# Results of tiles 46 and 47 in four small transfers, and the move of tile 40 in one piece

## The chip, the cores and the metric

The kernel runs on one core of one Trainium2 chip. The metric is the device time of one execution in microseconds (us). Before the change it is 209.26 us, the median of three runs (209.13 to 209.33). A core has five engines that work side by side, each with its own list of instructions: TensorE (PE in the profile, its weight loads PEld), VectorE (DVE), ScalarE (ACT), GpSimd (POOL) and SyncE (SP). They wait for each other by semaphores. Data go between the device memory and the core's own memory by transfers (DMA), which an engine issues and sixteen DMA engines carry out. In the core's own memory a tensor lies in 128 rows, the partitions.

## The reference

The kernel computes a batched matrix product, scaled, plus a second tensor:

```
batch, m, k, n = 16, 512, 1024, 768
out = (scale * np.matmul(x, weight) + add_value).astype(np.float32)
```

`x` is 16 x 512 x 1024, `weight` 1024 x 768, `add_value` and the output 16 x 512 x 768, all float32; `scale` is 0.1. The read inputs are 61.87 MB and the written output 25.17 MB.

## The kernel before

The 16 x 512 rows of `x` are one matrix of 8192 x 1024. It is worked on in 64 tiles of 128 rows. The tiles lie in three blocks (`BLOCKS`): tiles 0 to 23, 24 to 47 and 48 to 63. Inside a block, row p of every tile comes from partition p, and the rows of successive tiles follow each other in device memory: in the block of 24 tiles, partition p holds 24 successive rows of the matrix. A transfer of n successive tiles is therefore 128 rows, each of one unbroken stretch of n x 4096 bytes for `x` and n x 3072 bytes for `add_value` and the output.

`STREAM` lists the transfers in the order in which SyncE issues them. `x40+8` is the load of `x` for tiles 40 to 47, `a` stands for `add_value`, `w` for the weights and `o` for results that leave. `sync_engine` (the page's L106 is the wait, L113 to L118 the issues) waits before each one for the transfer eight places earlier (the eight semaphores in `lanes`), for the room it writes to, and for results for the results it sends. The last entry, `o60+4`, is issued after the section that holds all the other work (`tile_critical`), behind a barrier of all engines (L237).

- `xs` has room for 16 tiles of `x`. `ao` has room for 32 tiles; a tile of `add_value` is loaded there, the result is computed in place, and the result leaves from there.
- `mover` runs on ScalarE and on GpSimd, each with half of the work: in moves of four tiles it casts `x` to bf16 and brings it into `va`, which has two buffers. A move is eight casts of 32 x 1024 on each of the two engines. For the moves in `HALVED` it is sixteen casts of 32 x 512, first for two tiles and then for the other two, so that VectorE can begin on the first two sooner.
- `vector_engine` works in pairs of tiles. `turn(pair)` (L177) transposes a pair from `va` into `xt`; `finish(pair)` (L188) computes `scale * mm + a` into `ao` and counts `made` up by two. The order is finish of a pair, then turn of the pair two ahead, except after pairs 0 and 24.
- `tensor_engine` multiplies, per tile, eight pieces of 128 of the transposed `x` with the weights, in 512 and 256 columns (L232 and L207), into one of four places in `mm`.

Nothing is issued by GpSimd or by ScalarE before the change: all 28 transfers are SyncE's.

Of the kernel before, what the change touches and what calls it, by code (L numbers as in the profile page):

```python
# [7 lines left out]
P = 128  # L8
# [5 lines left out]
MM_BUFS = 4  # L14
XT_TILES = 4
LANES = 8
HALVED = (0, 1, 10)
TURN_FIRST = (0, 24)
VA_BUFS = 2
MOVE = 4  # L20

STREAM = """
    x0+4 w0+8 x4+8 a0+8 a8+8 x12+4 x16+8 a16+8 x24+8 a24+8 x32+8 o0+8 o8+8 a32+8 x40+8
    a40+8 x48+8 x56+4 o16+8 o24+8 a48+4 x60+4 a52+4 a56+8 o32+16 o48+4 o52+8 o60+4
"""


# [7 lines left out]
def kernel(  # L35
# [22 lines left out]
    def blocks(flat):  # L58
        return [(s, g, flat[P * s:P * (s + g), :].rearrange("(p t) n -> p t n", t=g))
                for s, g in BLOCKS]  # L60

    x_v, add_v, out_v = blocks(x_f), blocks(add_f), blocks(out_f)
    w_v = weight.rearrange("(p r) n -> p r n", p=P)

    def rows(view, s, n):
        for first, g, block in view:
            if first <= s and s + n <= first + g:
                return block[:, s - first:s - first + n, :]
        raise ValueError((s, n))
# [5 lines left out]
    ao = const.tile([P, A_SLOTS, N], fp32, name="ao")  # L75
    w_bf = const.tile([P, KJ, N], bf16, name="w_bf")
    RUN = K // 4
    va = [const.tile([P, MOVE, 4, RUN], bf16, name=f"va{i}") for i in range(VA_BUFS)]
    xt = const.tile([P, XT_TILES, KC, P], fp32, name="xt")
# [5 lines left out]
    by_act, by_pool, pool_go, turned, casts, done, made = (  # L85
        tc.alloc_semaphore(name)
        for name in ("by_act", "by_pool", "pool_go", "turned", "casts", "done", "made"))
    TURNED = MOVE * VA_BUFS
    MADE = TURNED + MM_BUFS

    def carriers(op, s, n):
        return [mark for (o, a, k), mark in zip(stream, landed)
                if o == op and a < s + n and s < a + k]

    def slots(op, s, n):
        ring = X_SLOTS if op == "x" else A_SLOTS
        k = s % ring
        assert k + n <= ring
        return slice(k, k + n)

    def engine(eng):
        known = {}

        def need(sem, value):
            if known.get(id(sem), 0) < value:
                eng.wait_ge(sem, value)  # L106
                known[id(sem)] = value

        return need

    def transfer(eng, op, s, n):
        if op == "w":
            return eng.dma_start(ao[:, W_SLOT + s:W_SLOT + s + n, :], w_v[:, s:s + n, :])  # L113
        if op == "x":
            return eng.dma_start(xs[:, slots(op, s, n), :], rows(x_v, s, n))  # L115
        if op == "a":
            return eng.dma_start(ao[:, slots(op, s, n), :], rows(add_v, s, n))  # L117
        return eng.dma_start(rows(out_v, s, n), ao[:, slots(op, s, n), :])  # L118

    def sync_engine(eng):  # L120
        need = engine(eng)
        for (op, s, n), (sem, mark) in zip(stream, landed):
            last = s + n
            if mark > 16:
                need(sem, mark - 16)
            if op == "x" and last > X_SLOTS:
                moved = 16 * -(-(last - X_SLOTS) // MOVE)
                need(by_act, moved)
                need(by_pool, moved)
            if op == "a":  # L130
                if s < W_SLOT + KJ <= A_SLOTS and last > W_SLOT:
                    need(casts, KJ)
                if s >= A_SLOTS:
                    for old in carriers("o", s - A_SLOTS, n):
                        need(*old)
            if op == "o":
                need(made, MADE + last)
            transfer(eng, op, s, n).then_inc(sem, 16)

    def mover(eng, copy, parity, count, go=None):  # L140
        need = engine(eng)
        if go is None:
            eng.preload_act_table(mybir.ActivationFunctionType.Copy)  # L143
        for q in range(MOVES):
            for mark in carriers("x", MOVE * q, MOVE):
                need(*mark)
            if q >= VA_BUFS:
                need(turned, TURNED + MOVE * (q - VA_BUFS + 1))
            if go is not None:
                eng.sem_inc(go, 1)  # L150
            k = MOVE * q % X_SLOTS
            src = xs[:, k:k + MOVE, :].rearrange("p i (b k) -> p i b k", b=4)
            step = MOVE // 2 if q in HALVED else MOVE
            for t in range(0, MOVE, step):
                for a in (parity, parity + 2):
                    for b in range(4):
                        copy(va[q % VA_BUFS][32 * b:32 * b + 32, t:t + step, a, :],  # L157
                             src[32 * a:32 * a + 32, t:t + step, b, :]).then_inc(count, step // 2)

    def vector_engine(eng):  # L160
        need = engine(eng)

        def cast_w(s, n):
            for mark in carriers("w", s, n):
                need(*mark)
            for h in range(s, s + n, 4):
                eng.tensor_copy(w_bf[:, h:h + 4, :], ao[:, W_SLOT + h:W_SLOT + h + 4, :]).then_inc(casts, 4)  # L167

        def turn(pair):
            move, half = divmod(pair, 2)  # L170
            moved = 16 * move + (8 * (half + 1) if move in HALVED else 16)
            need(by_act, moved)
            need(by_pool, moved)
            if pair > 1:
                need(done, 4 * (pair - 1))
            pairs = va[move % VA_BUFS][:, 2 * half:2 * half + 2, :, :].bitcast(fp32)
            eng.transpose(  # L177
                xt[:, 2 * half:2 * half + 2, :, :].rearrange("p i c (a m) -> p i c a m", a=4),
                pairs.rearrange("p i a (k c) -> p i c a k", c=KC),
            ).then_inc(turned, 2)  # L180

        def finish(pair):
            for mark in carriers("a", 2 * pair, 2):
                need(*mark)
            need(done, 4 * (pair + 1))
            a = ao[:, slots("a", 2 * pair, 2), :]
            q = 2 * (pair % 2)
            eng.scalar_tensor_tensor(  # L188
                a, mm[:, q:q + 2, 0:N], float(scale), a,
                op0=mybir.AluOpType.mult, op1=mybir.AluOpType.add).then_inc(made, 2)  # L190

        turn(0)
        for op, s, n in stream:
            if op == "w":
                cast_w(s, n)
        turn(1)
        for pair in range(T // 2):
            ahead = pair + 2 < T // 2
            if ahead and pair in TURN_FIRST:
                need(done, 4 * (pair + 1))  # L200
                turn(pair + 2)
            finish(pair)
            if ahead and pair not in TURN_FIRST:
                turn(pair + 2)
# [32 lines left out]
    with tc.tile_critical(no_gpsimd_drain=True):  # L237
        sync_engine(nc.sync)
        mover(nc.scalar, nc.scalar.copy, 0, by_act)
        mover(nc.gpsimd, nc.gpsimd.tensor_copy, 1, by_pool, pool_go)  # L240
        vector_engine(nc.vector)
        tensor_engine(nc.tensor)
# [36 lines left out]
```

## Time and profile before

| what | value |
|---|---|
| median of the runs | 209.26 us |
| the profiled execution | 209.87 us |
| its span, first to last instruction | 208.1 us |
| TensorE's granted clock, mean | 0.981 |
| busy: PE, DVE, ACT, POOL | 167.7, 122.9, 139.3, 139.9 us |
| DMA packets, bytes | 4035, 87.06 MB |
| rate over the span | 418 GB/s |

All rows of the profile are from one execution, in microseconds from the start of the span. In a row of the groups stand the line, engine, operation, output and inputs with their shapes, the count, then busy time, the mean of one in nanoseconds, and the idle time before them with what ended it. In a row of the timeline stand start, duration and what ran. A row of the stretches has the stretch, its length, the busy time of PE, PEld, DVE, ACT and POOL with the number of instructions, the granted clock of TensorE, the mean busy share of the sixteen DMA engines and the GB/s that they moved. A row of transfers has the size and the time from issue to landing; a landing is when all sixteen DMA engines have reported.

### The profile page before, as it was taken

The numbers are of one execution on the slowest core, as the hardware profiler recorded it, in microseconds if no ns is written. First come the engines' busy times: TensorE is split into PE (matmuls) and PEld (weight loads), VectorE is DVE, ScalarE is ACT, GpSimd is POOL, SyncE is SP. The second block draws the span as 40 slices with busy tenths as digits, with TensorE's granted clock in tenths as the row PEclk, the third lists the DMA queues.
The fourth block names the chain that finished last, engine by engine and source line by source line (L and its number), as shares of the span: only waits on it lengthen the run. The fifth ranks groups of instructions, "written<-read, shape, count | busy, mean of one in ns | idle before, by whom it ended". The sixth has DMA issues, their size and how long they took to land.

```text
span 208.1 us, 2174 instructions
## 1 busy us (share of the span) xinstructions
PE 167.7 (81%) x1008; PEld 50.4 (24%) x512; DVE 122.9 (59%) x66; ACT 139.3 (67%) x153; POOL 139.9 (67%) x156
## 2 busy tenths in 40 slices
PE   0001994969999999999999999994999999999500
PEld 0000231313333333333333333321333333333100
DVE  0037309646777777777777777738677759776300
ACT  2495199989799896969694069999998969000000
POOL 0399399999799997969694059999999979000000
PEclk9999999999999999999999999999999999999975
DMA  6999999999999999999999999999999999998993
GB/s 249 452 408 447 409 453 444 409 457 403 436 461 409 425 463 416 367 411 439 439 427 438 419 441 450 403 428 447 435 409 432 427 439 449 449 453 364 454 411 161
DMA packets 4035, 87.06 MB, mean 418 GB/s; under 512 B 448, under 2 KB 448, under 8 KB 448
## 3 DMA queue, kind: packets, MB, share of 16 engines
q1 hardware_dynamic: 4032, 87.03, 97.9%
q14 instruction: 3, 0.02, 0.0%
HBM read 61.87 MB, written 25.17 MB: 418 GB/s over the span
## 4 chain that ended last, share of the span: by engine, by line
DMA 43%; PE 25%; POOL 21%; issue 3%; DVE 2%; SPq 1%; POOLq 0%; DVEq 0%
DMA xs<-in_x_dram 31%; POOL va L157 21%; PE mm L232 16%; DMA out_dram<-ao 12%; PE mm L207 9%; DVE xt L177 1%; DVE ao L188 1%; SPq L115 0%; SPq L113 0%; SPq L117 0%; POOLq L150 0%; SPq L106 0%; DVEq L106 0%; SPq L274 0%; SPq L237 0%
## 5 line engine op out<-in xcount | busy, mean ns | idle before, releaser
L232 PE MATMUL mm<-w_bf,xt 128*128 128x512 bf16 x496 | 163.8, 382 | 26.9 <-DVE w_bf L167 19.8
L157 POOL CAST va<-xs 32x1024 bf16<-32x1024 f32 (+1 forms) x152 | 139.7, 919 | 36.8 <-DMA xs<-in_x_dram 22.4
L157 ACT CAST va<-xs 32x1024 bf16<-32x1024 f32 (+1 forms) x152 | 138.0, 908 | 36.6 <-DMA xs<-in_x_dram 23.4
L207 PE MATMUL mm<-w_bf,xt 128*128 128x256 bf16 x512 | 140.2, 274 | 0.8
L232 PEld LDWEIGHTS mm<-w_bf,xt 128*128 128x128 bf16 x512 | 50.4, 98 | 144.6 <-issue 138.7
L177 DVE STREAM_TRANSPOSE xt<-va 128x1024 f32<-128x1024 f32 x32 | 65.2, 2038 | 32.0 <-POOL va L157 30.6
L188 DVE SCALAR_TENSOR_TENSOR ao<-mm,ao 128x1536 f32<-128x1536 f32 x32 | 56.0, 1754 | 42.5 <-PE mm L207 39.4
L167 DVE CAST w_bf<-ao 128x3072 bf16<-128x3072 f32 x2 | 3.8, 1948 | 0.0
L143 ACT ACT_TABLE_LOAD x1 | 1.3, 1283 | 0.9 <-SPq L237 0.9
L260 POOL MEMSET const-float32-0.0<- 128x1 f32 x1 | 0.1, 98 | 0.2 <-issue 0.2
L260 POOL MEMSET const-bfloat16-1.0<- 128x1 bf16 x1 | 0.1, 101 | 0.0
L260 POOL MEMSET const-float32-1.0<- 128x1 f32 x1 | 0.1, 98 | 0.0
L260 POOL MEMSET const-uint8-127<- 128x1 uint8 x1 | 0.1, 98 | 0.0
## 6 DMA issues: line engine op xcount, KB each, us to landing
xs<-in_x_dram SPq DMA_DIRECT2D x6, 4096.0 KB, 20.8
ao<-in_add_value_dram SPq DMA_DIRECT2D x7, 3072.0 KB, 25.2
out_dram<-ao SPq DMA_DIRECT2D x5, 3072.0 KB, 24.8
xs<-in_x_dram SPq DMA_DIRECT2D x4, 2048.0 KB, 13.3
out_dram<-ao SPq DMA_DIRECT2D x1, 6144.0 KB, 33.9
ao<-in_weight_dram SPq DMA_DIRECT2D x1, 3072.0 KB, 14.1
ao<-in_add_value_dram SPq DMA_DIRECT2D x2, 1536.0 KB, 14.6
out_dram<-ao SPq DMA_DIRECT2D x2, 1536.0 KB, 19.8
```

The costliest lines, as they stand in the source:

```text
L143: eng.preload_act_table(mybir.ActivationFunctionType.Copy)
L157: copy(va[q % VA_BUFS][32 * b:32 * b + 32, t:t + step, a, :], src[32 * a:32 * a + 32, t:t + step, b, :]).then_inc(count, step // 2)
L167: eng.tensor_copy(w_bf[:, h:h + 4, :], ao[:, W_SLOT + h:W_SLOT + h + 4, :]).then_inc(casts, 4)
L177: eng.transpose(xt[:, 2 * half:2 * half + 2, :, :].rearrange("p i c (a m) -> p i c a m", a=4), pairs.rearrange("p i a (k c) -> p i c a k", ...
L188: eng.scalar_tensor_tensor(a, mm[:, q:q + 2, 0:N], float(scale), a, op0=mybir.AluOpType.mult, op1=mybir.AluOpType.add).then_inc(made, 2)
L207: return eng.add_instruction(mybir.InstMatmult(name=nc.get_next_instruction_name(), engine=eng.engine, ins=[eng.lower_ap(weights), eng.low ...
L232: eng.matmul(mm[:, q, 0:CUT], piece, w_bf[:, j, 0:CUT], **flags)
L260: nc = _bacc.Bacc("TRN2", target_bir_lowering=False, num_devices=1)
```

## The change

Three things are changed.

- The sixteen-tile transfer `o32+16` becomes `o32+14`. The results of tiles 46 and 47, 6,144 bytes in each of the 128 rows, leave in four transfers of their own (`SPREAD_ROWS`): rows 0 to 5 by SyncE, issued right after `o32+14`; rows 6 to 10, 11 to 115 and 116 to 127 by GpSimd, issued after its last move. Both wait until tile 47 is made.
- ScalarE, after its last move, waits for the landing of all four. So the barrier ahead of the last transfer is not passed before they have landed.
- `HALVED` loses move 10 (tiles 40 to 43), which is now made in eight casts on each engine in place of sixteen.

The row counts are chosen so that, of the 128 rows, engine 4 of the sixteen DMA engines gets three; a transfer of 128 rows gives it eight.

```
-HALVED = (0, 1, 10)
+HALVED = (0, 1)
+SPREAD = 46
+SPREAD_ROWS = (("SP", 6), ("Pool", 5), ("Pool", 105), ("Pool", 12))
...
-    a40+8 x48+8 x56+4 o16+8 o24+8 a48+4 x60+4 a52+4 a56+8 o32+16 o48+4 o52+8 o60+4
+    a40+8 x48+8 x56+4 o16+8 o24+8 a48+4 x60+4 a52+4 a56+8 o32+14 o48+4 o52+8 o60+4
...
+    spread_sem = [tc.alloc_semaphore(f"spread{i}") for i in range(len(SPREAD_ROWS))]
+
+    def spread(eng, name):
+        first = 0
+        for (by, n), sem in zip(SPREAD_ROWS, spread_sem):
+            if by == name:
+                eng.dma_start(rows(out_v, SPREAD, 2)[first:first + n],
+                              ao[first:first + n, slots("o", SPREAD, 2), :]).then_inc(sem, 16)
+            first += n
+        assert first == P
...
             transfer(eng, op, s, n).then_inc(sem, 16)
+            if op == "o" and last == SPREAD:
+                need(made, MADE + SPREAD + 2)
+                spread(eng, "SP")
...
+        if go is None:
+            for sem in spread_sem:
+                need(sem, 16)
+        else:
+            need(made, MADE + SPREAD + 2)
+            spread(eng, "Pool")
```

## The prediction

> **What bounds the kernel now.** I read the page's DMA rows first, then the busy time by stretch around the end, then SyncE's issues and waits.
>
> ```profile
> span 208.1 us, 2174 instructions
> q1 hardware_dynamic: 4032, 87.03, 97.9%
> q14 instruction: 3, 0.02, 0.0%
> DMA 43%; PE 25%; POOL 21%; issue 3%; DVE 2%; SPq 1%; POOLq 0%; DVEq 0%
> ```
>
> One queue, SyncE's, keeps the sixteen DMA engines busy for 97.9% of the span, 203.7 of 208.1 us. The chain of work names PE and GpSimd too, but a wait there ends in a transfer that would have run at that time anyway if the engines had other rows in store. The stretches say so:
>
> ```profile
> 100.00:150.00 50.00, 47.11 (x288) 14.19 (x145) 33.88 (x19) 37.01 (x44) 35.86 (x43) 1.00 1.01 435
> 200.00:205.00 5.00, 0.00 (x0) 0.00 (x0) 0.00 (x0) 0.00 (x0) 0.00 (x0) 0.54 0.91 388
> 205.54:205.60 0.06, 0.00 (x0) 0.00 (x0) 0.00 (x0) 0.00 (x0) 0.00 (x0) 0.50 0.48 205
> 205.60:205.75 0.15, 0.00 (x0) 0.00 (x0) 0.00 (x0) 0.00 (x0) 0.00 (x0) 0.50 0.00 0
> 205.75:205.80 0.05, 0.00 (x0) 0.00 (x0) 0.00 (x0) 0.00 (x0) 0.00 (x0) 0.50 0.57 246
> 205.80:205.95 0.15, 0.00 (x0) 0.00 (x0) 0.00 (x0) 0.00 (x0) 0.00 (x0) 0.50 0.00 0
> 205.95:206.00 0.05, 0.00 (x0) 0.00 (x0) 0.00 (x0) 0.00 (x0) 0.00 (x0) 0.50 0.57 246
> 206.00:206.40 0.40, 0.00 (x0) 0.00 (x0) 0.00 (x0) 0.00 (x0) 0.00 (x0) 0.50 0.00 0
> 206.40:206.45 0.05, 0.00 (x0) 0.00 (x0) 0.00 (x0) 0.00 (x0) 0.00 (x0) 0.50 0.57 246
> 206.45:207.25 0.80, 0.00 (x0) 0.00 (x0) 0.00 (x0) 0.00 (x0) 0.00 (x0) 0.50 0.00 0
> 204.50:204.75 0.25, 0.00 (x0) 0.00 (x0) 0.00 (x0) 0.00 (x0) 0.00 (x0) 0.50 0.59 246
> 204.75:205.00 0.25, 0.00 (x0) 0.00 (x0) 0.00 (x0) 0.00 (x0) 0.00 (x0) 0.50 0.13 49
> 0.00:5.00 5.00, 0.00 (x0) 0.00 (x0) 0.00 (x0) 1.28 (x1) 0.20 (x4) 1.00 0.64 233
> ```
>
> The last two columns are the DMA share and GB/s; a packet is counted whole in the stretch in which it starts. From 100 to 150 us the share is 1.01: no DMA engine rests. At the end the stretches are so short that single packets show. 246 GB/s over 0.05 us is 12.3 KB, one 12,288-byte row of the last transfer; 0.57 x 16 x 0.05 = 0.456 us is its time on its engine. The very last row starts in 206.40:206.45, so it ends near 206.88. Its engine's row before it started 0.46 us earlier, which is the one in 205.95:206.00. The row in 205.75:205.80 therefore belongs to another engine, whose next one would have started at 206.23 and did not: that engine ended near 206.23. The one in 205.54:205.60 is the last of a third engine, which ended near 206.03. So one engine ends 206.88 - 206.23 = 0.65 us behind the next, and everything after it waits for it:
>
> ```profile
> 0.94 0.38 SPq L115 DMA_DIRECT2D xs<-in_x_dram  x1
> 187.00 0.33 SPq L118 DMA_DIRECT2D out_dram<-ao  x1
> 197.66 0.33 SPq L118 DMA_DIRECT2D out_dram<-ao  x1
> SPq L274 <- DMA out_dram<-ao: 9.2, 1, 9.2
> out_dram<-ao SPq DMA_DIRECT2D x1, 1536.0 KB, 9.5
> out_dram<-ao SPq DMA_DIRECT2D x1, 3072.0 KB, 16.6
> ```
>
> The last transfer (tiles 60 to 63) is issued at 197.66 and lands 9.5 us later at 207.2, 0.3 after the last row's end; 0.9 us of closing work makes 208.1. Its rows queue behind tiles 52 to 59, issued at 187.00 and landed at 203.6, so its issue time is not what sets the end: the slowest engine's load is.
>
> **The change, part by part.** All sums are against the profiled execution, 209.87 us (span 208.10 and 1.77 around it); the median of the plain runs is 209.26, 0.61 less, and I carry the difference over to it. About 0.2% (0.42 us) is what a measurement of this kernel can tell from no change.
>
> *Fewer rows for one engine.* Each transfer has 128 rows, eight per engine. Tiles 46 and 47 are 6,144 bytes of each row; now each of those pieces is a row of its own. At 0.456 us per 12,288 bytes a piece costs 0.23 us. By the change's own words engine 4 gets three of them instead of eight: 5 x 0.23 = 1.15 us less. If engine 4 is the late one, it ends near 206.88 - 1.15 = 205.73, and the engine that ended at 206.23 becomes the last: a gain of 0.65 us at most. The trace doesn't number its DMA engines, so that they are the same one is an assumption.
>
> *Where the five rows go.* 125 pieces over fifteen engines is 8.33 each: at least five engines get nine, 0.23 us more. A dealing that fits is five on engines 0 to 4, 105 on all but engine 4 (seven each), twelve on 4 to 15, and SyncE's six on 0 to 5; then 0, 1, 2, 3 and 5 carry nine. The next-late and third-late engines (206.23 and 206.03) are among those with chances of about 5 in 15 each; then the gain falls to about 0.4 or less.
>
> *Cutting the rows.* What a shorter row costs shows here:
>
> ```profile
> q1 hardware_dynamic: 41, 1.84, 85.3%
> ...
> q1 hardware_dynamic: 39, 0.96, 113.9%
> q14 instruction: 2, 0.02, 2.4%
> ```
>
> The first row is 185 to 190 us, where the sixteen-tile transfer runs in 49,152-byte rows: 0.853 x 16 x 5 us / 1.84 MB = 37.1 us per MB, and a 12,288-byte row has 0.456 us / 0.0123 MB = 37.1 as well. So a cut within one queue costs nothing that I can see: lower bound 0. The upper bound comes from the other two rows, 58 to 60 us: two packets of another queue (instructions, 0.02 MB for three on the page, about 8 KB each) take 2.4% x 32 us / 2 = 0.38 us each where 37.1 us per MB makes 0.30. If each of eight rows out of GpSimd's queue cost those 0.08 extra, the next-late engine would end 0.64 us later and the gain would be gone. I take 0.15, nearer the first bound, since GpSimd's rows are ordinary rows of results: gain 0.65 - 0.15 = 0.50.
>
> *GpSimd's three issues and the new waits.*
>
> ```profile
> 158.72 0.38 SPq L118 DMA_DIRECT2D out_dram<-ao  x1
> 154.02 1.76 DVE L188 SCALAR_TENSOR_TENSOR ao<-mm,ao 128x1536 f32<-128x1536 f32 x1 [1.49 <-PE mm L207]
> 168.29 8.69 POOL L157 CAST va<-xs 32x1024 bf16<-32x1024 f32 x8 [0.90 <-DVE xt L177]
> 190.42 1.76 DVE L188 SCALAR_TENSOR_TENSOR ao<-mm,ao 128x1536 f32<-128x1536 f32 x1 [1.51 <-PE mm L207]
> 195.62 1.76 DVE L188 SCALAR_TENSOR_TENSOR ao<-mm,ao 128x1536 f32<-128x1536 f32 x1 [3.44 <-PE mm L207]
> ```
>
> SyncE's wait for tile 48 made (end of pair 23) is met at 155.78, before the issue at 158.72, so the extra issue adds some 0.4 us to SyncE there and nothing waits behind it: its next result is made later. GpSimd issues after its last cast, 168.29 + 8.69 = 176.98, with nothing queued behind. How long a GpSimd issue takes no row shows; from 0.33 (SyncE's) to a few us it changes nothing. ScalarE now waits for all four landings before the barrier ahead of the last transfer; that barrier closes today when the last result is made, 195.62 + 1.76 = 197.38. If the engines alternate between the queues, each of GpSimd's up to eight rows waits for one 43,008-byte row of the shortened transfer (1.60 us), so they are through by 177 + 1 + 8 x 1.83 = 193.6, ahead of 197.38: nothing. Instruction packets did get in at 58 to 60 us while the main queue had the engines at 113.9% (packets counted by their start), which speaks for alternation. [...]
>
> *Move of tile 40 whole.*
>
> ```profile
> L157 POOL CAST va<-xs 32x1024 bf16<-32x1024 f32 x104 | 107.6, 1034 | 12.9 <-DVE xt L177 5.7 <-DMA xs<-in_x_dram 1.2
> L157 POOL CAST va<-xs 32x512 bf16<-32x512 f32 x48 | 32.2, 670 | 24.0 <-DMA xs<-in_x_dram 21.3
> 121.75 45.64 POOL L157 CAST va<-xs 32x512 bf16<-32x512 f32 x48 [10.03 <-DMA xs<-in_x_dram]
> 127.17 2.05 DVE L177 STREAM_TRANSPOSE xt<-va 128x1024 f32<-128x1024 f32 x1 [0.25 <-POOL va L157]
> 130.36 1.76 DVE L188 SCALAR_TENSOR_TENSOR ao<-mm,ao 128x1536 f32<-128x1536 f32 x1 [1.15 <-PE mm L207]
> 141.26 2.01 DVE L177 STREAM_TRANSPOSE xt<-va 128x1024 f32<-128x1024 f32 x1 [3.91 <-POOL va L157]
> 143.33 0.39 PE L232 MATMUL mm<-w_bf,xt 128*128 128x512 bf16 x1 [2.68 <-DVE xt L177]
> ```
>
> Sixteen casts of 0.67 (10.7 us) become eight of 1.034 with 0.06 between (8.75 us): GpSimd ends the move at 130.5 instead of 132.4. But the first transpose, now at 127.17, must wait for the whole: 3.3 us later. PE, which ends pair 19 at 130.36, then waits until 132.6; two pairs of 5.2 us (195.62 - 190.42) take it to 143.0. The next move ends at 130.5 + 8.75 = 139.3, transposed by 141.6, so the 2.68 us stall at 143.33 goes and pair 22 starts at 143.0: 0.3 us earlier. Two stalls trade places; the gain of 0.3, or a loss up to about 2 us, is hidden by the rows in store. All but the late engines start their last row by 204.75:205.00 at the latest (one packet there, five in 204.50:204.75), the earliest some 0.6 before that; seven rows of 0.456 before that, they take up the last transfer at about 201, 3.3 us after its issue, and an issue needs about 1 us to start (of the first 5 us 36% is idle, 1.8 us, and the first issue stands at 0.94). Past that cover each us would count. Eight casts less and three issues more also leave GpSimd's program shorter, so I expect no fourth instruction packet.
>
> **The sum.** 209.87 - 0.65 + 0.15 = 209.37 for the profiled execution, 208.76 for the median: 0.24% faster.
>
> **The rivals.**
>
> *The gain is eaten (209.0).* As above, but the next-late engine carries nine pieces or GpSimd's rows cost more: 0.65 - 0.15 - 0.23 = 0.27 us, 208.99; with 0.64 for the queue and 0.23 for the row it ends at 209.48. For it: only 0.65 us separate first from second, and 0.2 second from third.
>
> *Engine 4 isn't the late one (209.4).* Then the late engine keeps eight or gets nine pieces: 209.26 + 0.15 to 209.26 + 0.38. The change wouldn't do what it is dealt for. The trace can't exclude it; against it only that one engine stands out so clearly by 0.65.
>
> *Every dealing starts at the first engine (209.87, slower).* If the 105 rows go seven each to engines 0 to 14, the five to 0 to 4 and the twelve to 0 to 11, then with SyncE's six engine 4 has 1 + 1 + 7 + 1 = 10 pieces, two more than before: 2 x 0.23 + 0.15 = 0.61 us, 209.87. It decides from two pieces on one late engine. [...]
>
> *GpSimd's rows starve (212, slower).* If an engine served the second queue only once the first is empty, the rows would wait for tiles 52 to 59, landed at 203.6, and the barrier with them; the last transfer, issued near 203.9, needs about 1 us to start, 8 x 0.456 = 3.65 of data and 0.3 to land: 208.9 plus 0.9, span 209.8 to 211, so 211 to 212. It decides once these landings pass 199 or so. The instruction packets speak against it.
>
> **How the numbers follow.** Main case 0.58, its own range 208.4 to 209.0 (0.46 faster by over 0.2%, 0.12 within). Gain eaten 0.13, within. Wrong engine 0.14: 0.09 within, 0.05 slower. Dealing from the first engine 0.09, slower. Starved 0.04 and something unlisted 0.02, slower. Together faster 0.46, same 0.34, slower 0.20. Predicted 208.76; the range goes from 208.4 (the late engine further behind in plain runs) to 209.9, which takes in all but the starved case and the upper part of the dealing.
>
> **What would show it.** Right: the last rows of the last transfer end within some 0.4 us of each other and near 206.4, GpSimd's transfers land before 197, the barrier still closes when the last result is made, and PE's stall sits before pair 20 instead of pair 22. Wrong: again one engine alone after 206.5 (wrong engine or dealing), landings from GpSimd after 197, a DMA share under 0.95 between 178 and 200, or a fourth instruction packet.

## The result: 0.6% slower

The changed kernel takes 210.69 us (median of seven runs, 210.32 to 211.20) against 209.33 us for the kernel before (209.13 to 209.75, seven runs beside them): a ratio of 1.0062, 95% interval 1.0046 to 1.0079. The forecast was 208.76, with 208.4 to 209.9 as its range; the time lies above it.

The changed kernel's page, its span and DMA queues (packets, MB, share of sixteen engines' span). The profiled execution took 211.2 us and is the longest of the seven:

```profile
span 209.4 us, 2180 instructions
q1 hardware_dynamic: 4044, 86.28, 96.6%
q0 software_dynamic: 192, 0.75, 1.1%
q14 instruction: 3, 0.02, 0.0%
```

The DMA engines are still the bound: 97.7% of 209.4 us is 204.6 us a piece, 0.9 more than the 203.7 before, for the same bytes. The 192 packets of GpSimd's queue are 122 rows of 6,144 bytes and 70 packets of 4 bytes. GpSimd's one transfer of 128 rows, further down, has 144 packets, 16 more than rows, one for each engine; three transfers make 48 by that count, and 22 more stand without a row, of which more below.

The end, in stretches of the changed kernel (last two columns DMA share and GB/s, as before):

```profile
205.00:205.50 0.50, 0.00 (x0) 0.00 (x0) 0.00 (x0) 0.00 (x0) 0.00 (x0) 0.50 0.58 246
205.50:206.00 0.50, 0.00 (x0) 0.00 (x0) 0.00 (x0) 0.00 (x0) 0.00 (x0) 0.50 0.29 123
206.50:207.00 0.50, 0.00 (x0) 0.00 (x0) 0.00 (x0) 0.00 (x0) 0.00 (x0) 0.50 0.12 49
207.30:207.65 0.35, 0.00 (x0) 0.00 (x0) 0.00 (x0) 0.00 (x0) 0.00 (x0) 0.50 0.00 0
207.65:207.75 0.10, 0.00 (x0) 0.00 (x0) 0.00 (x0) 0.00 (x0) 0.00 (x0) 0.50 0.29 123
207.75:208.50 0.75, 0.00 (x0) 0.00 (x0) 0.00 (x0) 0.00 (x0) 0.00 (x0) 0.50 0.00 0
```

The last row starts in 207.65:207.75 and ends near 208.15, where it ended near 206.88 before. And the sixteen engines end less together: in 205.00:205.50 still ten rows start (0.58 x 16 x 0.5 / 0.456), where before all but three engines had started their last row by 205.

Where the time goes shows in the stretch from 188.5 to 193.5 us, first the kernel before, then the changed one:

```profile
q1 hardware_dynamic: 136, 1.81, 84.6%
```

```profile
q1 hardware_dynamic: 124, 1.31, 65.1%
q0 software_dynamic: 116, 0.50, 31.8%
```

Both move 1.81 MB in packets that start there. Before, they hold 0.846 x 16 x 5 = 67.7 us of the engines, 37.4 us per MB. After, they hold (0.651 + 0.318) x 80 = 77.5 us, 42.8 per MB: ten engine-us more for the same bytes, in the stretch in which the results of tiles 46 and 47 leave.

What the prediction had set beside the path behaves as it said. The issues by GpSimd, their landings, SyncE's last issue, and the transpose and PE at the whole move, in the changed kernel:

```profile
176.29 1.70 POOL L99 DMA_DIRECT2D out_dram<-ao  x3
out_dram<-ao POOLq DMA_DIRECT2D x1, 630.0 KB, 17.2
out_dram<-ao POOLq DMA_DIRECT2D x1, 72.0 KB, 17.8
out_dram<-ao POOLq DMA_DIRECT2D x1, 30.0 KB, 8.3
197.03 0.33 SPq L131 DMA_DIRECT2D out_dram<-ao  x1
130.21 2.02 DVE L199 STREAM_TRANSPOSE xt<-va 128x1024 f32<-128x1024 f32 x1 [3.17 <-POOL va L173]
132.29 0.39 PE L254 MATMUL mm<-w_bf,xt 128*128 128x512 bf16 x1 [1.91 <-DVE xt L199]
```

The three issues take 1.70 us together; the rows land by 195.8 at the latest (issued by 177.99, 17.8 at the longest), so the barrier doesn't wait for them, and the last transfer is issued at 197.03, 0.63 earlier than before. The prediction had them through by 193.6 (its own terms, 177 + 1 + 8 x 1.83, make 192.6); they are two to three us later, and still ahead of the barrier. PE's stall now stands ahead of pair 20, 1.91 us at 132.29.

### The profile page after: what moved, and what is told of

The parts are those of the page before. It is cut to its first block, busy times and chain, and to the rows that moved or that the text cites. A ratio compares the mean times of both kernels' runs of the same rounds, so it can differ in the third digit from the quotient of the medians.

```text
span 209.4 us, 2180 instructions
## 1 busy us (share of the span) xinstructions
PE 169.6 (81%) x1024; PEld 50.5 (24%) x512; DVE 122.8 (59%) x66; ACT 137.8 (66%) x145; POOL 140.5 (67%) x151
## 4 chain that ended last, share of the span: by engine, by line
PE 50%; DMA 23%; POOL 15%; DVE 4%; issue 2%; SPq 0%; DVEq 0%; POOLq 0%
PE mm L254 33%; DMA xs<-in_x_dram 23%; PE mm L229 17%; POOL va L173 15%; DVE xt L199 2%; DVE ao L210 2%; SPq L126 0%; SPq L128 0%; DVEq L119 0%; POOLq L166 0%; SPq L296 0%; SPq L119 0%; SPq L259 0%
## 5 line engine op out<-in xcount | busy, mean ns | idle before, releaser
L254 PE MATMUL mm<-w_bf,xt 128*128 128x512 bf16 x512 | 169.1, 383 | 25.2 <-DVE w_bf L189 19.9
L173 ACT CAST va<-xs 32x1024 bf16<-32x1024 f32 (+1 forms) x144 | 136.5, 948 | 37.4 <-DMA xs<-in_x_dram 23.0
L99 POOL DMA_DIRECT2D out_dram<-ao x3 | 1.7, 573 | 0.0
```

What stands on the lines that cost most here:

```text
L99: eng.dma_start(rows(out_v, SPREAD, 2)[first:first + n], ao[first:first + n, slots("o", SPREAD, 2), :]).then_inc(sem, 16)
L254: eng.matmul(mm[:, q, 0:CUT], piece, w_bf[:, j, 0:CUT], **flags)
```

## The experiments

Each kernel ran beside the kernel before; the ratios are to it. In the first four the cause is narrowed down by taking one part at a time. All but the first keep the move of tile 40 in two halves.

### The whole move alone

```
-HALVED = (0, 1, 10)
+HALVED = (0, 1)
```

> The kernel before with the move of tile 40 whole and nothing else. All theories but one: no change, 209.3 within 0.3 us, since the rows in store hide it; PE's stall moves from before pair 22 to before pair 20. The rival that blames the whole move: 210.3 or more.

209.38 us, ratio 1.0005 (0.9991 to 1.0019). The whole move is hidden.

### The four transfers alone

```
-HALVED = (0, 1)
+HALVED = (0, 1, 10)
```

(against the changed kernel)

> The four transfers for tiles 46 and 47 alone, the move of tile 40 still in two halves. If the loss is in the four transfers: 210.3 to 211.0, and between 188 and 194 us each MB again costs some 42 engine-us in place of 37. If it is the whole move: 209.3. If GpSimd's longer list of instructions fetches a fourth packet, that shows in the queue of instructions.

211.11 us, ratio 1.0076 (1.0058 to 1.0095): the loss is in the four transfers. From 188.5 to 193.5 us each MB costs 43.0 engine-us, as in the changed kernel. The page counts four instruction packets in place of three, but for the same bytes:

```profile
q14 instruction: 4, 0.02, 0.0%
```

The fourth is one of 40 bytes and 8 ns, 0.06 us after the start of the span; the kernel before and the changed kernel have the same one 0.07 to 0.08 us ahead of theirs. The packets of 8,192 bytes are three in each of them, so the longer list of GpSimd fetched nothing more. The intervals of this kernel and of the changed one (1.0062) overlap.

### One transfer of 128 rows by GpSimd, and one by SyncE

```
-SPREAD_ROWS = (("SP", 6), ("Pool", 5), ("Pool", 105), ("Pool", 12))
+SPREAD_ROWS = (("Pool", 128),)
```

> Tiles 46 and 47 leave in one transfer of 128 rows issued by GpSimd, eight rows per engine as in all others; the move in two halves. Theory D (the dealing costs: rows handed to engines that do not serve them in a 128-row transfer take longer, and five engines get a ninth): the cost goes, 209.3 to 209.6, and the price per MB stays near 37 engine-us. Theory Q (GpSimd's queue beside SyncE's costs): 210.3 or more, the price stays near 42.

> Tiles 46 and 47 leave in one transfer of 128 rows issued by SyncE right after the fourteen tiles; the move in two halves. Theories D and Q: 209.3 to 209.5, only the cut is left. If cutting a row in two is what costs: 210.3 or more.

GpSimd's takes 209.60 us, ratio 1.0009 (0.9996 to 1.0022); SyncE's (`("SP", 128)`) 209.72, 1.0014 (1.0001 to 1.0027). From 188.5 to 193.5 us of GpSimd's:

```profile
q1 hardware_dynamic: 136, 1.54, 72.1%
q0 software_dynamic: 94, 0.49, 23.3%
```

(0.721 + 0.233) x 80 / 2.03 = 37.6 us per MB, as before. So the cut and GpSimd's queue cost some 0.2 to 0.3 us (at most 0.6 by the ends of the intervals), not the 1.3 to 1.6 of the four transfers. Theory Q falls, and what is left of the two is theory D: how the rows are dealt to the engines.

### Eight transfers of 16 rows, neighbouring or every eighth

```
+SPREAD_ROWS = (("SP", 16),) * 8
...
-                eng.dma_start(rows(out_v, SPREAD, 2)[first:first + n],
-                              ao[first:first + n, slots("o", SPREAD, 2), :]).then_inc(sem, 16)
+                eng.dma_start(rows(out_v, SPREAD, 2)[i:P:8],
+                              ao[i:P:8, slots("o", SPREAD, 2), :]).then_inc(sem, 16)
```

(the last four lines in the second kernel alone; `i` counts the transfers from 0)

The two kernels ask whether it matters which rows the engines read at the same time.

> Tiles 46 and 47 leave in eight SyncE transfers of 16 neighbouring rows (0 to 15, 16 to 31, ...), one row per engine and eight rows per engine in all; no GpSimd transfer, no ninth row; move in two halves. [...] Theory N (the ninth row on late engines is all there is): no engine has nine, 209.3 to 209.9. [...]

> The same eight SyncE transfers of 16 rows, but each takes every eighth row (0, 8, 16, ... then 1, 9, 17, ...). [...] Theory N and a rival that blames the number of small transfers: the same time as with neighbouring rows.

Neighbouring rows: 211.44 us, ratio 1.0105 (1.0087 to 1.0123). Every eighth: 210.73 us, 1.0045 (1.0023 to 1.0067). Every engine has eight rows in both, as in SyncE's one transfer of 128 (the packets, strung together by engine as described under the marks below, show it). The stretch 188 to 192.5 us holds most of these rows; SyncE's 128 first, then neighbouring, then every eighth:

```profile
q1 hardware_dynamic: 235, 1.82, 95.7%
```

```profile
q1 hardware_dynamic: 310, 1.33, 96.0%
```

```profile
q1 hardware_dynamic: 330, 1.52, 89.9%
```

That is 0.957 x 72 / 1.82 = 37.9, 52.0 and 42.6 us per MB. The rows themselves, as the traces' packets have them:

```
kernel                            rows of 6,144 B   mean ns   longest ns
one transfer of 128, SyncE              128            234        253
one transfer of 128, GpSimd             128            234        247
eight of 16, neighbouring               128            367       1615
eight of 16, every eighth               128            276        879
changed kernel                          128            290        953
GpSimd 16 and 112                       128            264        751
read neighbouring, write eighth         128            370       1466
read eighth, write neighbouring         128            252        644
```

Engines that serve neighbouring rows at the same time slow each other: 367 ns in the mean in place of 234, and 1,615, seven times as long, at most. With every eighth row it is less, 276 ns. An engine's eight neighbouring rows make 8 x 0.367 = 2.9 us in place of 1.9, though 99 of the 128 still took no more than 240 ns. Theory N falls: without any ninth row the kernel is 1.05 and 0.45% slower. The number of small transfers can't be the whole cause either: it is eight in both kernels.

### Reading side or writing side

```
                 eng.dma_start(rows(out_v, SPREAD, 2)[i:P:8],
-                              ao[i:P:8, slots("o", SPREAD, 2), :]).then_inc(sem, 16)
+                              ao[16 * i:16 * i + 16, slots("o", SPREAD, 2), :]).then_inc(sem, 16)
```

(against every eighth row on both sides; the second kernel has the two index ranges the other way round)

> Eight SyncE transfers of 16 rows for tiles 46 and 47, each reading 16 neighbouring partitions and writing them to every eighth row of the output (so the rows of these two tiles land in the wrong places of the output; the work is the same); move in two halves. If the engines meet on the reading side, in the core's memory: as with neighbouring rows on both sides, 211.4, and rows of 6,144 bytes that take 0.35 us or more in the mean. If they meet on the writing side: as with every eighth row on both sides, 210.7, mean under 0.30.

> The opposite: each of the eight transfers reads every eighth partition and writes 16 neighbouring rows of the output (rows of tiles 46 and 47 in the wrong places). Reading side: 210.7, mean row under 0.30 us. Writing side: 211.4, mean row 0.35 us or more.

Reading neighbours: 211.60 us, ratio 1.0107 (1.0086 to 1.0128), rows of 370 ns in the mean. Writing neighbours: 210.73 us, 1.0072 with a wide interval (1.0023 to 1.0121), rows of 252 ns. The times alone don't decide it: the two intervals overlap, and the runs of the second kernel go from 209.55 to 212.19, for a reason that isn't known. By the rows, in one profile of each, it is the reading side, and the stretches 188 to 192.5 us say the same, read first, written second:

```profile
q1 hardware_dynamic: 301, 1.27, 94.8%
```

```profile
q1 hardware_dynamic: 347, 1.75, 97.2%
```

53.7 against 40.0 us per MB.

### GpSimd's transfers of 8, 105 and 9 rows, and an even dealing

```
-SPREAD_ROWS = (("SP", 6), ("Pool", 5), ("Pool", 105), ("Pool", 12))
+SPREAD_ROWS = (("SP", 6), ("Pool", 8), ("Pool", 105), ("Pool", 9))
```

> The changed dealing with GpSimd's transfers of 8, 105 and 9 rows: by the dealing that the prediction assumed it is then engine 7 that gets two rows, engine 4 gets nine, engines 0 to 3 and 5 nine as before; move in two halves, to be held against the same kernel with 5, 105 and 12. If relieving engine 4 is worth the 0.65 us that the prediction gave it, this is 0.4 to 0.9 us slower than that one's 211.1. If engine 4 is not the one that holds up the end, both are within 0.4 us of each other.

210.63 us, ratio 1.0056 (1.0040 to 1.0071): not slower than with 5, 105 and 12 (1.0076), if anything faster. This doesn't answer the question that it was run for. By the dealing that the marks below show, and that this kernel's own packets confirm, engine 4 has ten rows with 8, 105 and 9 as with 5, 105 and 12, and engine 7 has nine: neither kernel relieves either of them.

```
+SPREAD_ROWS = (("Pool", 16), ("Pool", 112))
```

> Two GpSimd transfers of 16 and 112 rows in place of four: eight rows for every engine (one and seven), but not the rows that an engine serves in a 128-row transfer; move in two halves. [...] Theory N: no ninth row, so 209.3 to 209.7, as with one transfer of 128.

210.27 us, ratio 1.0043 (1.0028 to 1.0058). From 188.5 to 193.5 us:

```profile
q1 hardware_dynamic: 117, 1.33, 63.6%
q0 software_dynamic: 92, 0.48, 27.5%
```

40.3 us per MB. Each engine again has eight rows, but dealt as one and seven (which of the 128 they are, the packets don't show), and that costs 0.34% more than the one transfer of 128 (1.0043 against 1.0009), 0.7 us. What having two transfers in place of one adds to that isn't separated here.

### Which engine gets the rows

Four small loads with a different row size each, added to the kernel before, mark the engines:

```
+MARKS = ((4, 256), (12, 512), (5, 768), (11, 1024))
...
+            need(by_act, 16 * MOVES)
+            need(by_pool, 16 * MOVES)
+            for i, ((n, size), sem) in enumerate(zip(MARKS, mark_sem)):
+                eng.dma_start(xs[0:n, i, 0:size], x_f[0:n, 0:size]).then_inc(sem, 16)
```

> The kernel before plus four small loads by GpSimd after its last move, of 4, 12, 5 and 11 rows with 1, 2, 3 and 4 KB a row, into room of x that is no longer used; ScalarE waits for them. By the dealing the prediction assumed they go to engines 0 to 3, 4 to 15, 0 to 4 and 5 to 15, so that engine 4 alone gets a row of 2 KB and one of 3 KB; followed back to back to the end of the last transfer, the rows tell where engine 4 ends. If engine 4 is the late one, it ends last, 0.3 us or more behind the next, and the kernel stays within 0.4 us of 209.4. If it isn't, another engine ends last.

> The same kernel once more for a second profile: whether the same engine ends last in both. If engine 4 is always the late one, it is last here too; if the order changes from one execution to the next, it isn't.

209.95 us, ratio 1.0021 (1.0010 to 1.0031), and 209.9 in the second one. The packets carry no engine's number. But in these traces a packet starts within some 4 ns of the end of the one before it on its engine, and every engine takes SyncE's transfers in the same order, eight rows of each, so they can be strung together, one string for each engine; in the first kernel's profile the strings carry these marks:

```
marks of the string     strings   ends of the last transfer, us
1, 2, 3 and 4 KB           4      207.15 206.20 206.14 205.15
2, 3 and 4 KB              1      206.63
2 and 4 KB                 6      205.23 205.15 205.01 205.01 204.96 204.91
2 KB                       1      205.00
none                       4      205.42 205.41 205.20 205.12
```

Had each dealing gone on where the last one ended, every engine would carry two marks and none would carry four. What is there is 4, 12, 5 and 11 rows dealt each from the first engine on. Numbered by that dealing, 0 to 3 have all four marks, 4 has 2, 3 and 4 KB, 5 to 10 have 2 and 4, 11 has 2, and 12 to 15 none. That is the rival "every dealing starts at the first engine". The string with engine 4's marks ends second to last here; last is one of engines 0 to 3. In the second profile the order is the same: one of 0 to 3 is last (206.68), and engine 4's string is second to last (206.46). The marks' own rows take 0.41 us on engines 0 to 3 and 0.37 on engine 4 (46, 84, 121 and 160 ns each in the mean). In both profiles four of these five strings end 0.7 us and more behind all the others, so the marks alone don't make them late.

The same question put to the time:

```
+MARKS = ((5, 1536),) * 4
...
+                eng.dma_start(xs[0:4 * n:4, 2 * i:2 * i + 2, :].rearrange("p a k -> p (a k)")[:, 0:size],
+                              x_v[0][2][0:n, 2 * i:2 * i + 2, :].rearrange("p a k -> p (a k)")[:, 0:size]).then_inc(sem, 16)
```

> The kernel before plus four loads by GpSimd after its last move, each of five rows of 6,144 bytes, into room of x that is no longer used (partitions 0, 4, 8, 12, 16); ScalarE waits for them. If every dealing starts at the first engine, engines 0 to 4 get four rows each, 4 x 0.23 = 0.92 us on the engines that also end last: 210.2 to 210.6. If a dealing goes on where the last one ended, they go to engines 0 to 4, 5 to 9, 10 to 14 and 15 to 3: one or two rows each, 0.23 to 0.46 us: 209.6 to 210.0.

> The same bytes in four loads of sixteen rows of 1,920 bytes (every eighth partition): every engine gets four of them by either dealing, 0.07 us each, 0.29 in all: 209.6 to 209.9. It is what the loads cost when their rows are dealt evenly.

Five rows: 210.46 us, ratio 1.0049 (1.0035 to 1.0062). Sixteen rows: 209.91, 1.0026 (1.0017 to 1.0034). The even loads cost 0.54 us, more than the 0.29 I gave them; the five-row loads cost another 0.5 for the same bytes. Spread over the engines by dealings that go on where the last one ended, they would have cost, as I estimate from 0.23 us a row, 0 to 0.17 more than the even ones; all on engines 0 to 4, 0.63. In the trace of the five-row loads five strings carry four rows each and eleven carry none, and those five end last (205.69 to 207.40).

## Why the prediction was wrong

**The step that failed is the first: "By the change's own words engine 4 gets three of them instead of eight."** It gets ten. GpSimd's three transfers were dealt from the first engine on: 5 rows to engines 0 to 4, 105 to engines 0 to 14, 12 to engines 0 to 11, and SyncE's six to 0 to 5, which makes 1 + 1 + 7 + 1 = 10 for engines 0 to 4, nine for 5, eight for 6 to 11, seven for 12 to 14 and none for 15. The changed kernel's own packets say the same. Five strings carry nine GpSimd rows and one of SyncE's, one carries eight and one, six carry eight, three seven and one none; a dealing that goes on where the last one ended would give no engine more than eight of GpSimd's. The 22 packets without a row are as many as the rows that are missing on engines without a share (11 + 7 + 4). The three strings that end last, at 206.8, 207.7 and 208.2, are among those five. So engine 4 wasn't relieved; it and the four beside it were loaded, and one of 0 to 3 ended last in both profiles with marks.

**The rival was there and had its price too low.** "Every dealing starts at the first engine" had 209.87: two pieces, 2 x 0.23, and 0.15. Measured are 1.36 us over the kernel before (210.69 - 209.33) in place of 0.61. The two pieces stand. What was mis-sized is the 0.15 of "Cutting the rows".

**"Cutting the rows": the bound was looked for in the wrong place.** I bounded it by row length (nothing; 234 ns in the mean and 253 at most in the two 128-row transfers bear that out) and by GpSimd's queue (at most 0.08 a row; one transfer of 128 by GpSimd costs 0.09%). Both bounds held, and neither is what costs. What costs is that engines which read the newly dealt rows at the same time slow each other: 290 ns in the mean in place of 234, up to 953, and other packets beside them get longer too (rows of 43,008 bytes up to 1.98 us in place of 1.59). That this happens on the reading side is shown with the eight transfers, and for this kernel inferred from them.

The changed kernel's trace gives the size on the engines that matter. The two strings that end last have ten rows each. The twenty rows take 7.12 us, where sixteen at 234 ns take 3.74: for each string 0.47 us for two rows more and 1.22 us for longer rows, in place of the 0.15. On each of the two a row of 43,008 bytes took longer than the usual 1.59 us as well, by 0.39 and 0.26. Together that is more than the 1.27 us by which the last row's end moved (206.88 to 208.15), because in the profile of before the last engine stood worse to begin with: at 176 us it had one row of 24,576 bytes (0.91 us) more to go than the last one here. So the longer rows are the larger part and the two rows more the smaller; how the 1.36 us of the medians divide isn't shown by one trace.

**The late engine.** That one engine ends 0.65 us behind was read rightly in that execution. That it was engine 4 was an assumption, and it speaks against it that engine 4 ended second to last in both profiles with marks, 0.5 and 0.2 us ahead of one of 0 to 3. So the rival "Engine 4 isn't the late one" was likely right as well, though the order of the engines in the kernel before can't be read. Whether relief of the late engine would bring anything isn't shown: a dealing from the first engine on can't pass over a low-numbered one, so no kernel tried it, the one with 8, 105 and 9 rows included.

**What held.** The whole move is free (1.0005), and its stall trades places with the other, at 132.29 where I had 132.6. There are three instruction packets, but that isn't owed to the whole move, since the kernels with the move in two halves fetch no more. The queues alternated: on the engine that ends last, a row of SyncE's (1.59 us) and a packet of GpSimd's (0.23 us for a row) take turns from 181.6 us on, and the rows of GpSimd landed by 195.8, so "GpSimd's rows starve" didn't happen. The barrier still closed with the last result. SyncE's extra issue delayed nothing behind it: its last transfer went out earlier than before.

## What to carry to other kernels

When rows are dealt by hand, find out first which DMA engine gets which: transfers with different row sizes showed it here in one profile, and a dealing that was right on paper loaded the very engine it should spare, ten rows in place of three. Keep to transfers of all 128 partitions: there a row of 6,144 bytes took 234 ns in the mean and 253 at most, and cutting one in two cost 0.1%, while 16 neighbouring rows at a time made rows up to seven times as long. In a kernel that the DMA engines bound, the end is the slowest engine's (here thirteen were done by 206.1 us and the last at 208.2), so what counts is the worst-loaded engine and not the mean.

## What the runs showed of the hardware that I had not expected

- A row's time depended on what the other engines read beside it: 234 ns for 6,144 bytes in a 128-row transfer, 367 in the mean and 1,615 at most with 16 neighbouring rows per transfer. By the rows of one profile each it is on the reading side (370 against 252 ns).
- GpSimd's transfers of 4, 12, 5 and 11 rows were each dealt from the first engine on, one row an engine, and so were the 105 rows of the changed kernel, seven each on fifteen engines.
- An engine without a share of a GpSimd transfer still had packets of 4 bytes in place of the rows: 22 in the changed kernel and 32 with the marks, as many as the missing rows.
- Four small loads by GpSimd cost 0.54 us when dealt evenly (0.36 to 0.71), where their bytes make 0.29. The rows of 1,920 bytes took 79 ns in the mean, 0.32 us for an engine's four; where the rest comes from isn't shown.
